# Holding VectorE's side work behind the newest low part of the weights, from the output product to the end of a decoder layer

## The chip, the cores and the metric

The kernel runs on one core of one Trainium2 chip. The metric is the device time of one execution in microseconds (us). Before the change, three runs took 1912.0, 1913.61 and 1914.93 us; the median is 1913.61 us. One further execution was profiled; everything said of single instructions is from it.

## The reference, cut to what matters

One decoder layer on a sequence of 512 rows and 2048 columns, all in float32:

```python
h = rms_norm(x, norm1_g)
proj = h @ w_in                        # 2048 x 6160, feeds two kinds of attention
mix = concatenate([out_a, out_b])      # gated linear attention, dilated attention
x = x + mix @ w_out                    # the output product, 2048 x 2048
h2 = rms_norm(x, norm2_g)
x = x + (silu(h2 @ w_gate) * (h2 @ w_up)) @ w_down    # FFN, hidden size 5632
```

The change touches the last three lines: the output product, the two FFN products (called gate and up below) and the down product.

## The kernel before, in words

**Products in seven.** Two neighbouring 512-column blocks of a weight matrix form a pair, and each pair is computed with seven sub-products in place of eight (Strassen's scheme): PRODUCTS is P1, P5, P6, P3, P7, P2, P4. The activations enter as A11, A12, A21, A22 and as sums S1 to S4 of these; the weights enter as quarters a, b, c, d (512 KB each, loaded into tiles wa, wb, wc, wd). P1, P3 and P2 take one quarter as it is; P5, P6, P7 and P4 need a difference of two quarters, which VectorE makes (`Pair.source`, L298). Each sub-product runs over groups g of 256 rows: four in the output product, in gate and up, and in most of the down product, which is cut into three parts of 4, 4 and 3 groups. There are 2 pairs in the output product, 11 in gate and up, 6 in the down product.

**High and low parts.** TensorE multiplies in a rounded format (fp32r), so each operand is split into a high part (rounded copy) and a low part (the remainder). For weights, ScalarE makes the high part `wh` (L376) and VectorE the low part `wl` = source minus high (L380); both come from a pool with two buffers each (`hpool`). One item of the stream (one sub-product, one group) is twelve matmuls of 512 columns at L405: first eight with `wh`, then four with `wl`. The activations are split the same way into tiles called AA or AS (A11, A12, A22 and S1 to S4; 28 buffers in `apool`): ScalarE writes the high half (L198), VectorE the low half (L199, `Operand.split`).

**The stream.** `stream` walks all items. While it writes down item k it first writes the high part of item k+1, the weight sum of item k+2, the low part of item k+1 (and notes that instruction in `recent["low"]`), then the matmuls of item k; after the eighth matmul it calls `step()`, which releases a share of the background work: splits, sums of activations, loads. `later(n, fn)` puts a closing, a residual addition or a transpose n items further on.

**What sets the order.** Tile's scheduler places the instructions of PE (TensorE), ACT (ScalarE), DVE (VectorE), SP (the DMA queue of the sync engine) by its own estimate of when each can run; each engine then executes its list strictly in that order. `tc.issue_after(ins)` adds one constraint: what is traced inside the block stands behind `ins` on its own engine. The kernel before uses it for the closings of the first pairs of the input product (`behind=True`, L337) and for the sums in `sums_job` (L1464 to L1474).

**Side work on VectorE** from the output product on, beside weight sums and low parts: low halves of splits (L199), sums of activation rows (L223 to L236 in `Operand.build`, L1231 to L1241, L1321 in `kept_job`), closings that add a PSUM accumulator to a saved seed (L339 without and L343 with a row scale), residual additions (`residual`, L1287, L1290, L1293, with the old x loaded into tiles q and k at L1283), the product of silu(gate) and up (L1432), and 32x32-block transposes of the result (L1404). PE also transposes tiles with an identity matrix (L1099) in the output product.

Of the kernel before, what the change touches and what calls it, by code (L numbers as in the profile page):

```python
# [131 lines left out]
def block_kernel(ctx: ExitStack, tc: tile.TileContext, ins, out):  # L132
# [52 lines left out]
    recent = {}  # L185
    done = set()


    class Operand:

# [5 lines left out]
        def split(self, name, g, src):  # L196
            a = apool.tile([P, 2, 2, 256], F32R, name=nm("A" + name), tag="A")
            nc.scalar.copy(a[:, :, 0, :], src)  # L198
            nc.vector.tensor_tensor(  # L199
                a[:, :, 1, :], src, a[:, :, 0, :].bitcast(F32), op=ALU.subtract  # L200
            )
            self.t[name, g] = a

        def half_split(self, which, name, g, src):
# [10 lines left out]
        def build(self, g, r11, r21, r12, r22):  # L215

            get = lambda r: r() if callable(r) else r
            tt = nc.vector.tensor_tensor
            r11 = get(r11)
            self.split("A11", g, r11)  # L220
            yield
            r22 = get(r22)
            self.split("A22", g, r22)  # L223
            yield
            r21 = get(r21)
            tt(r22, r21, r22, op=ALU.add)
            self.split("S1", g, r22)
            yield
            tt(r21, r11, r21, op=ALU.subtract)
            tt(r11, r22, r11, op=ALU.subtract)  # L230
            self.split("S2", g, r11)
            yield
            r12 = get(r12)
            tt(r11, r12, r11, op=ALU.subtract)
            self.split("S4", g, r11)
            yield  # L236
            self.split("S3", g, r21)
            yield
            self.split("A12", g, r12)
            yield  # L240
# [29 lines left out]
    def halves(t):  # L270
        return t.rearrange("p (b a) -> p b a", b=2)
# [1006 lines left out]
    def residual(tiles, acc_, rows, c0, src, late=False):  # L1278

        res, adds = [], []  # L1280
        for m in range(2):
            r = work(("q", "k")[m])
            load(r, src(rows[m], c0))  # L1283
            if late:
                res.append(tiles[m])
                adds.append(
                    lambda m=m, r=r: nc.vector.tensor_tensor(tiles[m], tiles[m], r, op=ALU.add)  # L1287
                )
            elif tiles is None:
                nc.vector.tensor_tensor(halves(r), unfolded(acc_[m]), halves(r), op=ALU.add)  # L1290
                res.append(r)
            else:
                nc.vector.tensor_tensor(tiles[m], tiles[m], r, op=ALU.add)  # L1293
                res.append(tiles[m])
        return res, adds

    kept_n = {}
# [1 line left out]
    def kept_job(op, kept):  # L1299
        tt = nc.vector.tensor_tensor  # L1300
        sums = {
            "S3": ("t1", "t0", "t1", ALU.subtract), "S2": ("t1", "r1", "t1", ALU.subtract),
            "S1": ("t0", "t1", "t0", ALU.add), "S4": ("t1", "r0", "t1", ALU.subtract),
        }
        parts = {"A11": "t0", "S3": "t1", "S1": "t0", "S2": "t1", "A12": "r0", "S4": "t1", "A22": "r1"}
        have = lambda n: (n[0], int(n[1])) in kept
        for word in KEPT.split():
            for one in word.split("+"):
                name, *g = one.split(".")
                split = name in parts and one[0] != "="  # L1310
                name = name.strip("=")
                g = int(g[0])
                needs = [parts[name]] if split else sums[name][:3]
                while not all(have(n) for n in needs):
                    yield
                at = lambda n: kept[n[0], int(n[1])][g - 2]
                if split:
                    op.split(name, g, at(parts[name]))
                else:
                    d, a, b, how = sums[name]  # L1320
                    tt(at(d), at(a), at(b), op=how)  # L1321
            yield

    def final_out(second):
# [51 lines left out]
    opn = Operand(4)  # L1376
    tops = [xn_d[2], xn_d[3], xn_d[6], xn_d[7]]
    bots = [xn_d[0], xn_d[1], xn_d[4], xn_d[5]]
    pair(opm, rows_mix, ocol(0), ocol(512), final_out(0), scripted(step, OUT))
    pair(opm, rows_mix, ocol(1024), ocol(1536), final_out(1), paced([1] * 28))  # L1380


    rows_n = [(512, 0), (768, 256), (1536, 1024), (1792, 1280)]
# [15 lines left out]
    def turned_store(tiles, half, j):  # L1399

        dst = turned_d[j][half].rearrange("q (k i) n -> i (q k) n", i=32)
        for m in range(2):
            d = work(("oT", "PT")[m])
            nc.vector.transpose(d, tiles[m])  # L1404
            for a in range(4):
                store(
                    dst[:, :, m * P + 32 * a : m * P + 32 * a + 32],
# [7 lines left out]
    def final_ffn(j):  # L1415
        ups = {}

        def final(half, which, tiles, acc_):
# [4 lines left out]
            for m in range(2):  # L1423
# [5 lines left out]
                else:  # L1429
                    s = tiles[m]  # L1430
                    nc.scalar.activation(s, s, AF.Silu)
                nc.vector.tensor_tensor(up[m], up[m], s, op=ALU.mult)  # L1432
            def rest():
                if j in turned_d:
                    turned_store(up, half, j)
# [72 lines left out]
    for j in range(11):  # L1508
        pair(
            opn, rows_n, w_gate[:, j], w_up[:, j], final_ffn(j),  # L1510
            paced(paces.get(j, ())), tok_scale, before=lambda j=j: before_ffn(j),
        )


# [45 lines left out]
    for i in range(3):  # L1560
        g0 = 4 * i
        rows_d = [(512 * (g0 + g), 512 * (g0 + g) + 256) for g in range(opd[i].groups)]
        for np_ in range(2):
            lead = np_ == 1 and i < 2
            pair(
                opd[i], rows_d, w_down[:, 2 * np_], w_down[:, 2 * np_ + 1],
                final_down(i, np_), paced(renewal if lead else closing if i < 2 else ()),
                before=(
                    (lambda i=i: background.append(down_jobs(i + 1))) if lead
                    else (lambda: later(6, lambda: background.extend(last_sums))) if (i, np_) == (0, 0) else None  # L1570
# [63 lines left out]
```

## Time and profile before

| | us |
|---|---|
| median of three runs | 1913.61 |
| the profiled execution's own time | 1913.48 |
| its span, first to last instruction | 1911.7 |
| PE busy | 1897.4 |
| DVE busy | 1675.1 |
| ACT busy | 1070.1 |

The output product's first matmul stands at about 545 us, gate and up run from about 702 to 1500 us, the down product from there to 1908 us. In rows of the profile, PE is TensorE's matmuls, PEld its weight loads, DVE VectorE, ACT ScalarE, and SPq the queue that issues DMAs. In a timeline a row has the start, the duration (of the whole row where xcount is over 1), engine, line, operation, tiles and, in brackets, how long the engine was idle before it and what released it. A row of windows has, for each engine, busy time and the number of instructions in brackets. A matmul's start is exact; its end is modelled, and neighbours overlap.

### The profile page before, as it was taken

The numbers are of one execution on the slowest core, as the hardware profiler recorded it, in microseconds if no ns is written. First come the engines' busy times: TensorE is split into PE (matmuls) and PEld (weight loads), VectorE is DVE, ScalarE is ACT, GpSimd is POOL, SyncE is SP. The second block draws the span as 40 slices with busy tenths as digits, with TensorE's granted clock in tenths as the row PEclk, the third lists the DMA queues.
The fourth block names the chain that finished last, engine by engine and source line by source line (L and its number), as shares of the span: only waits on it lengthen the run. The fifth ranks groups of instructions, "written<-read, shape, count | busy, mean of one in ns | idle before, by whom it ended". The sixth has DMA issues, their size and how long they took to land.

```text
span 1911.7 us, 25301 instructions
## 1 busy us (share of the span) xinstructions
PE 1897.4 (99%) x9002; PEld 1644.5 (86%) x9002; DVE 1675.1 (88%) x1956; ACT 1070.1 (56%) x1567; POOL 13.1 (1%) x22
## 2 busy tenths in 40 slices
PE   9999999999999999999999999999999999999999
PEld 7888888888888888888888888888888888888887
DVE  8898797778799999988888888888889989979987
ACT  8654564666776665544544544444546546546543
POOL 0000010000000000000000000000000000000000
PEclk9999999999999999999999999999999999999999
DMA  9637455444536563465465465464466776855761
GB/s 341 209 111 250 147 168 181 144 152 157 188 122 226 162 218 124 124 182 167 136 193 170 121 196 157 129 198 147 141 198 200 213 263 213 278 203 182 237 221 66
DMA packets 246806, 345.73 MB, mean 181 GB/s; under 512 B 107718, under 2 KB 154607, under 8 KB 246680
## 3 DMA queue, kind: packets, MB, share of 16 engines
q1 hardware_dynamic: 246392, 343.99, 55.9%
q8 instruction: 70, 1.15, 0.2%
q14 instruction: 56, 0.46, 0.1%
q10 hardware_dynamic: 288, 0.14, 0.0%
HBM read 286.10 MB, written 60.31 MB: 181 GB/s over the span
## 4 chain that ended last, share of the span: by engine, by line
PE 81%; DVE 7%; DMA 3%; issue 3%; ACT 1%; SPq 0%; DVEq 0%; ACTq 0%
PE acc L405 76%; DVE wl L380 3%; DVE wa L298 1%; PE bank L1003 1%; PE bank L979 1%; DMA q<-y_d 1%; DVE AS L199 1%; PE bank L996 0%; DVE AA L199 0%; DVE seed L1287 0%; DMA wd<-in_w_down 0%; PE bank L1099 0%; PE bank L918 0%; PE bank L901 0%; DMA xn_d<-oT 0%
## 5 line engine op out<-in xcount | busy, mean ns | idle before, releaser
L405 PE MATMUL acc<-wh,AS 128*128 128x512 f32 x3008 | 710.9, 379 | 0.0
L405 PEld LDWEIGHTS acc<-wh,AS 128*128 128x128 f32 x3008 | 568.3, 189 | 81.4 <-ACT wh L376 0.9
L376 ACT CAST wh<-wa 128x1024 fp32r<-128x1024 f32 x376 | 394.4, 1049 | 403.8 <-PE acc L405 367.3
L405 PE MATMUL acc<-wh,AA 128*128 128x512 f32 x2256 | 533.5, 379 | 0.2 <-ACT wh L376 0.2
L380 DVE TENSOR_TENSOR wl<-wa,wh 128x1024 fp32r<-128x1024 f32 x376 | 456.5, 1216 | 57.9 <-ACT wh L376 46.2
L405 PEld LDWEIGHTS acc<-wh,AA 128*128 128x128 f32 x2256 | 426.2, 189 | 61.0 <-ACT wh L376 0.6
L405 PE MATMUL acc<-wl,AS 128*128 128x512 f32 x1504 | 393.7, 384 | 4.3 <-DVE wl L380 4.2
L405 PEld LDWEIGHTS acc<-wl,AS 128*128 128x128 f32 x1504 | 280.8, 189 | 53.0 <-DVE wl L380 12.0
L405 PE MATMUL acc<-wl,AA 128*128 128x512 f32 x1128 | 295.1, 384 | 0.3
L405 PEld LDWEIGHTS acc<-wl,AA 128*128 128x128 f32 x1128 | 211.1, 189 | 34.3 <-DVE wl L380 3.4
L376 ACT CAST wh<-wb 128x1024 fp32r<-128x1024 f32 x94 | 98.6, 1049 | 121.1 <-PE acc L405 118.9
L376 ACT CAST wh<-wc 128x1024 fp32r<-128x1024 f32 x94 | 98.6, 1049 | 119.6 <-PE acc L405 103.9
L376 ACT CAST wh<-wd 128x1024 fp32r<-128x1024 f32 x94 | 98.6, 1049 | 90.4 <-PE acc L405 75.4
L380 DVE TENSOR_TENSOR wl<-wd,wh 128x1024 fp32r<-128x1024 f32 x94 | 114.4, 1219 | 32.1 <-ACT wh L376 28.8
L298 DVE TENSOR_TENSOR wa<-wc,wa 128x1024 f32<-128x1024 f32 x94 | 114.3, 1220 | 30.9 <-DMA wc<-in_w_gate 19.1
L380 DVE TENSOR_TENSOR wl<-wc,wh 128x1024 fp32r<-128x1024 f32 x94 | 114.5, 1219 | 26.7 <-ACT wh L376 26.1
L380 DVE TENSOR_TENSOR wl<-wb,wh 128x1024 fp32r<-128x1024 f32 x94 | 114.3, 1216 | 9.0 <-ACT wh L376 7.3
L298 DVE TENSOR_TENSOR wb<-wd,wb 128x1024 f32<-128x1024 f32 x94 | 114.1, 1216 | 0.4
L298 DVE TENSOR_TENSOR wa<-wb,wa 128x1024 f32<-128x1024 f32 x94 | 113.6, 1211 | 0.8
L298 DVE TENSOR_TENSOR wa<-wd,wa 128x1024 f32<-128x1024 f32 x94 | 112.9, 1215 | 0.1
L343 DVE SCALAR_TENSOR_TENSOR seed<-acc,rs,seed 128x512 f32<-128x512 f32 x96 | 70.3, 745 | 15.8 <-PE acc L405 14.6
L324 ACT ACTIVATE seed<-acc,rs 128x512 f32<-128x512 f32 x96 | 60.8, 682 | 5.1 <-PE acc L405 5.1
(319 smaller groups left out, 1264.5 us busy)
## 6 DMA issues: line engine op xcount, KB each, us to landing
wa<-in_w_gate SPq DMA_DIRECT2D x44, 512.0 KB, 3.3
wb<-in_w_up SPq DMA_DIRECT2D x44, 512.0 KB, 6.0
wd<-in_w_up SPq DMA_DIRECT2D x44, 512.0 KB, 4.3
wc<-in_w_gate SPq DMA_DIRECT2D x44, 512.0 KB, 3.3
wa<-in_w_in SPq DMA_DIRECT2D x24, 512.0 KB, 4.9
wc<-in_w_in SPq DMA_DIRECT2D x24, 512.0 KB, 3.4
wb<-in_w_in SPq DMA_DIRECT2D x24, 512.0 KB, 5.2
wd<-in_w_in SPq DMA_DIRECT2D x24, 512.0 KB, 4.9
```

The costliest lines, as they stand in the source:

```text
L199: nc.vector.tensor_tensor(a[:, :, 1, :], src, a[:, :, 0, :].bitcast(F32), op=ALU.subtract)
L298: nc.vector.tensor_tensor(src, other, src, op=ALU.subtract)
L324: nc.scalar.activation(halves(t), unfolded(src[m]), AF.Copy, scale=self.scale(half, m))
L343: nc.vector.scalar_tensor_tensor(halves(seed[m]), unfolded(src[m]), self.scale(half, m), halves(seed[m]), op0=ALU.mult, op1=ALU.add,)
L376: nc.scalar.copy(high[k], sources[k])
L380: recent["low"] = nc.vector.tensor_tensor(low[k], sources.pop(k), high[k].bitcast(F32), op=ALU.subtract).ins
L405: nc.tensor.matmul(p.dst[prod][m], a[:, jj, hl, m * P : (m + 1) * P], folded(w[i][:, jj, :]), start=fresh and g == 0 and i == 0 and jj == ...
L979: nc.tensor.matmul(lp[:, :n], qh[:, b * P : (b + 1) * P], kh[:, :n], start=True, stop=True)
L1003: nc.tensor.matmul(op, vh[:, k, :], lgs[b][:, k * P : (k + 1) * P], start=(k == 0), stop=(k == b))
```

## The change

A helper `low_first()` opens `tc.issue_after(recent["low"])`: what is traced inside stands on VectorE behind the newest low part of weights traced so far, that is, the one of the next item. It is put around the low halves of all splits, the sums of activation rows in `Operand.build` and `kept_job`, the residual additions, the product with silu and the transposes of the result. All pairs of the output product, of gate and up and of the down product get `behind=True`, which does the same for their closings. No instruction is added or removed; durations and shapes stay.

```diff
+    def low_first():
+
+        return tc.issue_after(recent["low"])
...
         def split(self, name, g, src):
             a = apool.tile([P, 2, 2, 256], F32R, name=nm("A" + name), tag="A")
             nc.scalar.copy(a[:, :, 0, :], src)
-            nc.vector.tensor_tensor(
-                a[:, :, 1, :], src, a[:, :, 0, :].bitcast(F32), op=ALU.subtract
-            )
+            with low_first():
+                nc.vector.tensor_tensor(
+                    a[:, :, 1, :], src, a[:, :, 0, :].bitcast(F32), op=ALU.subtract
+                )
...
-            tt(r22, r21, r22, op=ALU.add)
+            with low_first():
+                tt(r22, r21, r22, op=ALU.add)
...
             if late:
                 res.append(tiles[m])
-                adds.append(
-                    lambda m=m, r=r: nc.vector.tensor_tensor(tiles[m], tiles[m], r, op=ALU.add)
-                )
-            elif tiles is None:
-                nc.vector.tensor_tensor(halves(r), unfolded(acc_[m]), halves(r), op=ALU.add)
-                res.append(r)
+
+                def add(m=m, r=r):
+                    with low_first():
+                        nc.vector.tensor_tensor(tiles[m], tiles[m], r, op=ALU.add)
+
+                adds.append(add)
             else:
-                nc.vector.tensor_tensor(tiles[m], tiles[m], r, op=ALU.add)
-                res.append(tiles[m])
+                with low_first():
+                    if tiles is None:
+                        nc.vector.tensor_tensor(
+                            halves(r), unfolded(acc_[m]), halves(r), op=ALU.add
+                        )
+                    else:
+                        nc.vector.tensor_tensor(tiles[m], tiles[m], r, op=ALU.add)
+                res.append(r if tiles is None else tiles[m])
...
-    pair(opm, rows_mix, ocol(0), ocol(512), final_out(0), scripted(step, OUT))
-    pair(opm, rows_mix, ocol(1024), ocol(1536), final_out(1), paced([1] * 28))
+    pair(opm, rows_mix, ocol(0), ocol(512), final_out(0), scripted(step, OUT), behind=True)
+    pair(opm, rows_mix, ocol(1024), ocol(1536), final_out(1), paced([1] * 28), behind=True)
...
-            nc.vector.transpose(d, tiles[m])
+            with low_first():
+                nc.vector.transpose(d, tiles[m])
...
-                nc.vector.tensor_tensor(up[m], up[m], s, op=ALU.mult)
+                with low_first():
+                    nc.vector.tensor_tensor(up[m], up[m], s, op=ALU.mult)
...
-            paced(paces.get(j, ())), tok_scale, before=lambda j=j: before_ffn(j),
+            paced(paces.get(j, ())), tok_scale, before=lambda j=j: before_ffn(j), behind=True,
...
                 final_down(i, np_), paced(renewal if lead else closing if i < 2 else ()),
+                behind=True,
```

The same wrapping is put around the other sums of `Operand.build` and those of `kept_job`. The scheduler works out all lists anew, so other instructions move too. Three places on VectorE follow (numbers after a tile's name tell its instances apart).

The first place is the first pair of the down product, about 1509 to 1518 us. On VectorE there stood before, from one low part to the third after it:

```order
L380 TENSOR_TENSOR wl_2342_13047<-wa_2336_13021,wh_2340_13043 128x1024
L1404 STREAM_TRANSPOSE oT_2350_13086<-seed_2244_12564 128x512
L298 TENSOR_TENSOR wa_2329_12996<-wb_2353_13104,wa_2329_12996 128x1024
L380 TENSOR_TENSOR wl_2349_13076<-wa_2341_13045,wh_2347_13071 128x1024
L298 TENSOR_TENSOR wa_2336_13021<-wb_2360_13130,wa_2336_13021 128x1024
L298 TENSOR_TENSOR wa_2341_13045<-wb_2364_13151,wa_2341_13045 128x1024
L1404 STREAM_TRANSPOSE PT_2351_13092<-seed_2250_12590 128x512
L380 TENSOR_TENSOR wl_2354_13107<-wa_2322_12961,wh_2352_13102 128x1024
```

And on VectorE between the same low parts now (L388 is the low part, L306 the weight sum, L204 the low half of a split, L1420 the transpose):

```order
L388 TENSOR_TENSOR wl_2342_13047<-wa_2336_13021,wh_2340_13043 128x1024
L204 TENSOR_TENSOR AA12_2344_13059<-T_2326_12985,AA12_2344_13059 128x2x256
L204 TENSOR_TENSOR AA12_2346_13064<-qT_2331_13008,AA12_2346_13064 128x2x256
L388 TENSOR_TENSOR wl_2349_13076<-wa_2341_13045,wh_2347_13071 128x1024
L1420 STREAM_TRANSPOSE oT_2350_13086<-seed_2244_12564 128x512
L306 TENSOR_TENSOR wa_2329_12996<-wb_2353_13104,wa_2329_12996 128x1024
L388 TENSOR_TENSOR wl_2354_13107<-wa_2322_12961,wh_2352_13102 128x1024
```

Two weight sums and a transpose left the stretch ahead of wl_2354, and two splits that stood further ahead came in.

The second place is the last pair, about 1850 to 1859 us, where tiles q and k hold rows loaded by DMA for the residual addition. On VectorE before:

```order
L380 TENSOR_TENSOR wl_2894_15953<-wa_2888_15928,wh_2892_15949 128x1024
L298 TENSOR_TENSOR wa_2888_15928<-wb_2903_16001,wa_2888_15928 128x1024
L1290 TENSOR_TENSOR q_2900_15987<-acc_2821_15543,q_2900_15987 128x512
L380 TENSOR_TENSOR wl_2899_15975<-wa_2893_15951,wh_2897_15971 128x1024
L1290 TENSOR_TENSOR k_2901_15990<-acc_2822_15544,k_2901_15990 128x512
L298 TENSOR_TENSOR wa_2893_15951<-wb_2906_16020,wa_2893_15951 128x1024
L380 TENSOR_TENSOR wl_2904_16004<-wa_2898_15973,wh_2902_15999 128x1024
```

And on VectorE there now (L1297 and L1303 are residual additions):

```order
L388 TENSOR_TENSOR wl_2894_15953<-wa_2888_15928,wh_2892_15949 128x1024
L1297 TENSOR_TENSOR seed_2839_15626<-seed_2839_15626,q_2890_15941 128x512
L306 TENSOR_TENSOR wa_2888_15928<-wb_2903_16001,wa_2888_15928 128x1024
L388 TENSOR_TENSOR wl_2899_15975<-wa_2893_15951,wh_2897_15971 128x1024
L1297 TENSOR_TENSOR seed_2843_15647<-seed_2843_15647,k_2891_15943 128x512
L306 TENSOR_TENSOR wa_2893_15951<-wb_2906_16020,wa_2893_15951 128x1024
L1303 TENSOR_TENSOR q_2900_15987<-acc_2821_15543,q_2900_15987 128x512
L388 TENSOR_TENSOR wl_2904_16004<-wa_2898_15973,wh_2902_15999 128x1024
```

The additions to the seeds now follow two or three low parts later; the loads into q and k can be issued only after these additions have read the tiles, and the addition q_2900 stands directly ahead of wl_2904.

The third place is the third item of the output product, about 549 to 556 us, where the attention's last tiles (cr) are still being finished. On VectorE before:

```order
L380 TENSOR_TENSOR wl_980_5213<-wa_969_5174,wh_978_5209 128x1024
L1136 SCALAR_TENSOR_TENSOR og_962_5141<-acc_759_4177,rs1_102,og_962_5141 128x512
L199 TENSOR_TENSOR AS3_983_5236<-top_963_5144,AS3_983_5236 128x2x256
L298 TENSOR_TENSOR wa_966_5156<-wb_988_5263,wa_966_5156 128x1024
L1147 TENSOR_TENSOR cr_981_5223<-cr_981_5223,og_962_5141 128x512
L1234 TENSOR_TENSOR top_886_4756<-qT_971_5186,top_886_4756 128x512
L298 TENSOR_TENSOR wa_969_5174<-wb_996_5301,wa_969_5174 128x1024
L1147 TENSOR_TENSOR cr_982_5224<-cr_982_5224,og_962_5141 128x512
L380 TENSOR_TENSOR wl_986_5247<-wa_979_5211,wh_984_5243 128x1024
L380 TENSOR_TENSOR wl_989_5266<-wa_985_5245,wh_987_5261 128x1024
```

And on VectorE now, up to the same addition cr_982 (L1155):

```order
L388 TENSOR_TENSOR wl_980_5213<-wa_969_5174,wh_978_5209 128x1024
L1144 SCALAR_TENSOR_TENSOR og_962_5141<-acc_759_4177,rs1_102,og_962_5141 128x512
L204 TENSOR_TENSOR AS3_983_5236<-top_963_5144,AS3_983_5236 128x2x256
L388 TENSOR_TENSOR wl_986_5247<-wa_979_5211,wh_984_5243 128x1024
L1155 TENSOR_TENSOR cr_981_5223<-cr_981_5223,og_962_5141 128x512
L306 TENSOR_TENSOR wa_966_5156<-wb_988_5263,wa_966_5156 128x1024
L388 TENSOR_TENSOR wl_989_5266<-wa_985_5245,wh_987_5261 128x1024
L1155 TENSOR_TENSOR cr_982_5224<-cr_982_5224,og_962_5141 128x512
```

Both low parts now stand ahead of cr_982, which PE's transposes of cr wait for; in PE's list six of these eight transposes stand between two of the four matmuls with wl_986 and the other two.

More of the change, by code (lines that the diff above doesn't have):

```diff
@@ L225, in build @@
             r21 = get(r21)
-            tt(r22, r21, r22, op=ALU.add)
+            with low_first():
+                tt(r22, r21, r22, op=ALU.add)
             self.split("S1", g, r22)
             yield
-            tt(r21, r11, r21, op=ALU.subtract)
-            tt(r11, r22, r11, op=ALU.subtract)
+            with low_first():
+                tt(r21, r11, r21, op=ALU.subtract)
+                tt(r11, r22, r11, op=ALU.subtract)
             self.split("S2", g, r11)
@@ L233, in build @@
             r12 = get(r12)
-            tt(r11, r12, r11, op=ALU.subtract)
+            with low_first():
+                tt(r11, r12, r11, op=ALU.subtract)
             self.split("S4", g, r11)
@@ L1320, in kept_job @@
                     d, a, b, how = sums[name]
-                    tt(at(d), at(a), at(b), op=how)
+                    with low_first():
+                        tt(at(d), at(a), at(b), op=how)
             yield
@@ L1403, in turned_store @@
             d = work(("oT", "PT")[m])
-            nc.vector.transpose(d, tiles[m])
+            with low_first():
+                nc.vector.transpose(d, tiles[m])
             for a in range(4):
@@ L1431, in final @@
                     nc.scalar.activation(s, s, AF.Silu)
-                nc.vector.tensor_tensor(up[m], up[m], s, op=ALU.mult)
+                with low_first():
+                    nc.vector.tensor_tensor(up[m], up[m], s, op=ALU.mult)
             def rest():
```

## The prediction

> **What bounds the kernel now.** I read the page first, then the windows of the stages, the waits, and the timeline where time is lost. TensorE is the bound:
>
> ```profile
> span 1911.7 us, 25301 instructions
> PE 1897.4 (99%) x9002; PEld 1644.5 (86%) x9002; DVE 1675.1 (88%) x1956; ACT 1070.1 (56%) x1567; POOL 13.1 (1%) x22
> ```
>
> PE counts as busy for 99% of the span, so its busy time can't show what is lost. The number of matmuls in a stretch can. These windows count the L405 matmuls alone:
>
> ```profile
> 566.00:667.00 101.00, 97.21 (x441) 82.28 (x441) 1.00 0.56 182
> 895.00:1440.00 545.00, 545.00 (x2526) 477.24 (x2526) 1.00 0.54 163
> 1457.00:1540.00 83.00, 81.18 (x373) 69.75 (x372) 1.00 0.71 222
> 1610.00:1682.00 72.00, 71.68 (x326) 60.40 (x325) 1.00 0.72 242
> 1755.00:1790.00 35.00, 34.92 (x161) 29.70 (x161) 1.00 0.82 276
> 1855.00:1885.00 30.00, 29.77 (x137) 25.25 (x136) 1.00 0.13 42
> ```
>
> In gate and up (895 to 1440) 2526 matmuls take 545 us, 0.2158 us each, and nothing is lost there. At that pitch the 373 matmuls of 1457 to 1540 need 80.5 us of 83: 2.5 lost. In the same way 72 − 326 x 0.2158 = 1.6, 35 − 34.7 = 0.3, and 30 − 29.6 = 0.4. In the output product, 101 − 441 x 0.2158 = 5.8, and from this come PE's 32 transposes:
>
> ```profile
> 566.00:667.00 101.00, 4.15 (x32) 3.74 (x32) 1.00 0.56 182
> 554.45 1.04 PE L1099 MATMUL bank<-mats,cr 128*128 128x128 f32 x8
> 555.31 1.13 PE L405 MATMUL acc<-wl,AA 128*128 128x512 f32 x4
> PEld acc L405 <- DVE wl L380: 4.4, 7, 1.1
> PEld acc L405 <- DVE wl L380: 8.9, 21, 1.4
> ```
>
> By their busy time these cost 4.15 us. By the two timeline rows eight of them put the next matmul off by 0.86 us (554.45 to 555.31), which is 3.5 for the 32; I go by the starts, so 5.8 − 3.5 = 2.3 are lost. The last two rows (waits of 566 to 720 us, and of 1440 to 1905) say to whom: the weight loads of TensorE waited 7 and 21 times for a low part. With one more stall near 718 (below), some 7 to 8 us of 1911.7 are open to this change, under half a per cent. About 0.2% (3.8 us; the three runs lie 2.9 apart) is what a measurement here can tell from no change.
>
> How such a stall arises is seen in VectorE's timeline of the first down pair, and TensorE's beside it:
>
> ```profile
> 1508.54 0.68 DVE L1432 TENSOR_TENSOR seed<-seed,k 128x512 f32<-128x512 f32 x1
> 1509.14 1.22 DVE L380 TENSOR_TENSOR wl<-wa,wh 128x1024 fp32r<-128x1024 f32 x1
> 1510.28 0.70 DVE L1404 STREAM_TRANSPOSE oT<-seed 128x512 f32<-128x512 f32 x1
> 1510.91 1.18 DVE L298 TENSOR_TENSOR wa<-wb,wa 128x1024 f32<-128x1024 f32 x1
> 1512.01 1.21 DVE L380 TENSOR_TENSOR wl<-wa,wh 128x1024 fp32r<-128x1024 f32 x1
> 1513.14 2.35 DVE L298 TENSOR_TENSOR wa<-wb,wa 128x1024 f32<-128x1024 f32 x2
> 1515.41 0.70 DVE L1404 STREAM_TRANSPOSE PT<-seed 128x512 f32<-128x512 f32 x1
> 1516.04 2.31 DVE L380 TENSOR_TENSOR wl<-wa,wh 128x1024 fp32r<-128x1024 f32 x2
> ...
> 1517.27 0.92 PE L405 MATMUL acc<-wl,AS 128*128 128x512 f32 x3 [1.01 <-DVE wl L380]
> ```
>
> VectorE has no gap: back to back an operation on 1024 columns takes 1.13 us (1509.14 to 1510.28), one on 512 takes 0.60 (1508.54 to 1509.14), a transpose 0.63. Two weight sums and a transpose stand ahead of the low part at 1516.04, for which PE is idle 1.01 us. An item of twelve matmuls takes 12 x 0.2158 = 2.59 us; VectorE's share of it, with a weight sum, is 2 x 1.13 = 2.27. The 0.3 left over is too little for any other operation, so splits and additions push the low parts back until an item without a sum comes.
>
> **The change part by part.** No instruction is added; what moves is which of them stands ahead of a low part. In the first place shown of the order, between wl_2342 and wl_2354 there stood a transpose, a sum, a low part, two sums and a transpose: 0.63 + 1.13 + 1.13 + 2.27 + 0.63 = 5.8 us. Now two splits, a low part, a transpose and one sum stand there: 2 x 0.6 + 1.13 + 0.63 + 1.13 = 4.1. That is 1.7 us earlier, more than the 1.01 of idle PE. What left goes behind, to 1540 and later, where nothing is lost. The same holds for the other low parts that PE waits for from 1457 to 1682 and near 1783: less or equal work ahead of each. I take all but 0.2 of the 2.5, about half of what TensorE waited for ScalarE instead (the row below): **−2.3** (bounds −2.5 and −1.0, if the moved work fills the next items). The windows 1610 and 1755: **−1.9**, before what follows.
>
> ```profile
> PEld acc L405 <- ACT wh L376: 0.4, 1, 0.4
> ```
>
> The splits, sums and transposes that now wait have users far off: an A operand is made one pair ahead, dozens of items before its first matmul, so a delay of a few items costs nothing. Closings free PSUM tiles; they move by one item at most of their product's four. FFN: weight sums move ahead of low parts at each pair's start, by 1.13 us; VectorE's idle before low parts covers that:
>
> ```profile
> DVE wl L380 <- ACT wh L376: 62.8, 60, 1.4
> ```
>
> (60 waits from 740 to 1440 us.) Cost nothing; if the cover were gone, up to 1.13 us in each of 11 pairs.
>
> The residual additions are another matter. A load into q or k can be issued only when the addition before it has read the tile, so a held addition delays the next load, on SP's queue, and whatever stands behind it there; and an addition whose rows haven't landed stops VectorE's whole list. The last pair shows it already:
>
> ```profile
> 1849.01 2.40 DVE L380 TENSOR_TENSOR wl<-wa,wh 128x1024 fp32r<-128x1024 f32 x2
> 1849.56 0.40 SPq L1283 DMA_DIRECT2D q<-y_d  x1
> 1850.01 1.32 SPq L1283 DMA_DIRECT2D k<-y_d  x1
> 1851.44 1.22 DVE L298 TENSOR_TENSOR wa<-wb,wa 128x1024 f32<-128x1024 f32 x1
> 1854.12 0.69 DVE L1290 TENSOR_TENSOR q<-acc,q 128x512 f32<-128x512 f32 x1 [1.46 <-DMA q<-y_d]
> 1859.26 1.03 PE L405 MATMUL acc<-wl,AA 128*128 128x512 f32 x4
> q<-y_d SPq DMA_DIRECT2D x15, 256.0 KB, 5.0
> DMA to landing us min/median/max: 2.2/5.0/6.9
> ```
>
> The addition waits 1.46 us for its rows. In the new order (second place) the addition to seed_2839 comes after wl_2894 (the second of the two low parts in the first row, which end at 1851.4), so it ends at 1852.0. SP then issues a store, and the load of q_2900 near 1852.6, not at 1849.56. By the median of 5.0 it lands near 1857.6; q_2900 ends 0.68 later and wl_2904, next in the list, 1.13 after that, at 1859.4. PE needs it at 1859.26. That is 0.2 lost, up to 2.1 with the longest landing of 6.9 and nothing with 2.2; and k_2901 repeats part of it. Against this stand the 0.4 lost there now. I take **0** here (bounds −0.4 and +2.0) and **+0.5** for the same thing at the end of the other tight pair, near 1655 us (bounds 0 and +1.5). Elsewhere the items have room.
>
> The Trainium skill ("DMA: Bandwidth & Descriptors", section on the anatomy of one DMA) prices a DMA on GpSimd's path at 2.0 us plus bytes over 436 GB/s. As an estimate from that page 256 KB would take 2.6 us, half the median of the rows above; by it these two terms would be −0.4 and 0, and the sum 0.9 lower.
>
> **Output product.** VectorE's rows near 630 to 643:
>
> ```profile
> 633.92 0.69 DVE L199 TENSOR_TENSOR AA<-r,AA 128x512 fp32r<-128x512 f32 x1 [1.40 <-ACT AA L198]
> ...
> 642.02 1.22 DVE L380 TENSOR_TENSOR wl<-wa,wh 128x1024 fp32r<-128x1024 f32 x1
> 643.29 0.91 PE L405 MATMUL acc<-wl,AS 128*128 128x512 f32 x3 [0.62 <-DVE wl L380]
> ...
> 718.87 1.13 PE L405 MATMUL acc<-wl,AS 128*128 128x512 f32 x4 [0.75 <-DVE wl L380]
> ```
>
> At 633.92 VectorE idled 1.40 us, because a split stood at the head of its list and its rows had not landed; ten instructions without a gap later PE lacks a low part. The new list puts that split behind the next low part, so the idle time goes, but a weight sum comes in place of the split (1.13 for 0.60: 0.5 more ahead of each low part): 0.9 gained. Of the 0.75 at 718 and the rest of the 2.3 I count 0.4: **−1.3** (bounds −2.3 and 0).
>
> Its start is worse:
>
> ```profile
> 551.48 1.04 ACT L376 CAST wh<-wa 128x1024 fp32r<-128x1024 f32 x1
> 553.45 0.68 DVE L1147 TENSOR_TENSOR cr<-cr,og 128x512 f32<-128x512 f32 x1
> ```
>
> Today cr_982 (553.45) is ready when PE comes to its eight transposes at 554.45 (the row near the top). In the third place of the order wl_986 and wl_989, 2 x 1.13, stand ahead of it; a sum (1.13) and a sum of rows (0.6) leave, so it comes some 0.5 us later by work, and wl_986 must wait for a cast that ends at 552.5, where another 0.5 to 1.5 goes. PE would wait up to 1.5 us. I take **+0.9** (bounds −0.5 and +2.0; it lies nearer to the cast's row, which is fixed by when TensorE frees the buffer).
>
> **The sum** against the profiled execution: −2.3 − 1.9 + 0.5 + 0 − 1.3 + 0.9 = −4.1, so 1913.48 − 4.1 = 1909.4 us. The median of the runs is 0.13 above the profiled time, which I leave out. The end of the kernel does not move: the last closings stand ahead of PE's last matmuls before and after.
>
> **The rivals.**
>
> *The stall moves (no change).* Where VectorE has no gap, putting work behind one low part puts it ahead of the next; only idle time that goes or weight sums that move out of the stretch are a real gain. For it: from 636 to 643 VectorE is full before and after. Against it: after 1540 and 1682 there is room. Then −1.2 at 1457, −0.8 at 1610 and 1755, 0 in the output product but the +0.9: −1.1, 1912.4 us. Chance 0.27.
>
> *Late residual rows (slower).* The additions held behind low parts make five pairs of the down product wait at their last product:
>
> ```profile
> L1290 DVE TENSOR_TENSOR q<-acc,q x5: 678/683/691, 1580.3 to 1854.1; 128x512 f32<-128x512 f32 x5
> ```
>
> At 2.1 us each (landing after 6.9) five pairs cost 10.5; with the −2.3, −1.9 and −0.4 gained elsewhere that is +5.9, 1919.4 us. It decides from 1.7 us per pair on. Against it: only one pair in five waited for such rows before (1.46). Chance 0.09.
>
> *Rows land early (faster).* All landings near the minimum of 2.2 us: −2.3 − 1.9 − 0.4 − 1.3 + 0.9 = −5.0, 1908.5 us. This is what the page's rule would give. Against it: the median of 5.0. Chance 0.12.
>
> *All waits go (faster).* The start costs nothing either, and the output product gains its full 2.3 and the 0.75 at 718: −2.5 − 1.9 − 0.4 − 3.1 = −7.9, 1905.6 us. Chance 0.08.
>
> **How the numbers follow.** My forecast, 1909.4, has 0.44; its own bounds straddle 1909.8, the 0.2% line, and I count 0.32 of it as faster and 0.12 as no change. Faster: 0.32 + 0.12 + 0.08 = 0.52. Within 0.2%: 0.12 + 0.27 = 0.39. Slower: 0.09. The range reaches down to the case in which all waits go, 1905.6, and up past the moved stall (1912.4) by the upper bound of the start (2.0 − 0.9 = 1.1) and 0.5 of the last pair's 2.0: 1914.0; it leaves out most of the slower case.
>
> **What would show it.** Right: the count of L405 matmuls in the stretch of the first down pair at the pitch of 0.2158, and few waits of PEld for wl after 1440; the gap at 1517 gone. The start: PE waiting for the cr addition between 553 and 557. The last pair: VectorE's wait for q rows longer than 1.46. Wrong: PEld's waits for wl unchanged in sum but at other items, or waits for DMA rows in several down pairs.

## The result, and the profile after

The changed kernel is slower. Its median over six runs is 1927.41 us (1924.94 to 1930.93), that of the kernel before, run beside it, 1912.8 us, 14.6 us less. The ratio, formed from the means, is 1.0074 with a 95% interval of 1.006 to 1.0089. The forecast was 1909.4, with a range that ended at 1914.0. The profiled execution took 1926.13 us.

The page of the changed kernel, first the span, then each engine's busy time with its instructions:

```profile
span 1924.3 us, 25274 instructions
PE 1902.8 (99%) x9002; PEld 1642.9 (85%) x9002; DVE 1676.0 (87%) x1956; ACT 1069.2 (56%) x1567; POOL 13.3 (1%) x22
```

The work is the same (DVE 1676.0 us against 1675.1); the span has 12.6 us more. The windows of the matmuls (now L413), over about the same stretches as those shown of before:

```profile
566.20:668.40 102.20, 97.93 (x441) 82.28 (x441) 1.00 0.55 179
895.55:1441.55 546.00, 546.00 (x2530) 477.15 (x2529) 1.00 0.55 163
1457.70:1544.20 86.50, 83.42 (x381) 70.81 (x379) 1.00 0.70 213
1618.40:1690.00 71.60, 71.33 (x323) 60.63 (x324) 1.00 0.72 249
1765.10:1801.00 35.90, 34.84 (x159) 29.79 (x160) 1.00 0.86 283
```

At 0.2158 us a matmul the output product lost 102.2 − 95.2 = 7.0, less 3.5 for the transposes, that is 3.5 us (2.3 before). Gate and up still lost nothing. The first down pair lost 86.5 − 82.2 = 4.3 (2.5 before), the other two windows 1.9 and 1.6 (1.6 and 0.3). From 1440 us on the weight loads waited:

```profile
PEld acc L413 <- DVE wl L388: 16.9, 26, 1.8
PEld acc L413 <- ACT wh L384: 4.6, 6, 1.4
```

Waits for low parts, which the change was to shorten, went from 8.9 to 16.9 us, and waits for ScalarE's casts from 0.4 to 4.6.

A second reading needs no windows: the start of the same matmul (the k-th at that line) in both traces, and how far the two drift apart. It gives for each stretch what the profiled execution lost (+) or gained (−) against the profiled execution of before, in us:

| kernel | 93–707 | 707–1449 | 1449–1586 | 1586–1907 |
|---|---|---|---|---|
| changed | +1.6 | +0.4 | +3.3 | +7.8 |
| splits not held | +0.3 | +0.4 | 0.0 | +4.9 |
| residual additions not held | +0.2 | +0.6 | +4.3 | +7.0 |
| neither held | −0.1 | +0.3 | +0.7 | +0.2 |
| only splits held | +0.7 | −0.6 | +6.7 | +3.2 |
| changed, operand's rows loaded once | +2.6 | +0.3 | −0.9 | +7.8 |
| changed, residual rows loaded once | +5.6 | +0.3 | +3.0 | +1.8 |
| changed, both kinds of rows loaded once | +0.7 | +0.3 | −1.0 | −0.9 |
| before, both kinds of rows loaded once | −1.5 | −0.7 | −1.7 | −0.9 |
| nothing of the down product held | +1.0 | +0.5 | −1.0 | +0.7 |
| only the last pair of gate and up | −1.7 | −0.2 | −0.7 | 0.0 |

(Times of before; the kernels below the first row are those of the experiments.) Of the 13 us, 11 are lost in the down product. The first column is the least sure: "before, both kinds of rows loaded once" and the last row have the order of before on TensorE, VectorE and ScalarE up to 1440 us, and still they show −1.5 and −1.7 there. So the profiled execution of before seems to have been some 1.6 us late in that stretch itself, and the column shows the cost of the change there too small by about as much.

Nor does one execution always stand for its kernel. The profiled one of "splits not held" took 1918.65 us against a median of 1922.45, that of "residual additions not held" 1926.64 against 1920.28, that of "residual rows loaded once" 1924.49 against 1919.25. The table says where time is lost; the medians say how much.

**What happened there.** One place in the first down pair, in the changed kernel: ScalarE, VectorE, the DMA queue and TensorE, in order of time.

```profile
1473.03 0.61 ACT L202 CAST AS<-qT 128x512 fp32r<-128x512 f32 x1
1483.84 0.68 DVE L204 TENSOR_TENSOR AS<-qT,AS 128x512 fp32r<-128x512 f32 x1
1484.10 1.06 ACT L384 CAST wh<-wc 128x1024 fp32r<-128x1024 f32 x1 [1.54 <-DMA wa<-in_w_down]
1484.55 0.33 SPq L1208 DMA_DIRECT2D qT<-S_d  x1
1488.98 0.62 ACT L202 CAST AS<-qT 128x512 fp32r<-128x512 f32 x1 [3.81 <-DMA qT<-S_d]
...
1490.21 1.04 ACT L384 CAST wh<-wc 128x1024 fp32r<-128x1024 f32 x1
1491.30 1.99 PE L413 MATMUL acc<-wh,AA 128*128 128x512 f32 x8 [1.02 <-ACT wh L384]
```

and the same load in the kernel before:

```profile
1473.96 0.68 DVE L199 TENSOR_TENSOR AS<-qT,AS 128x512 fp32r<-128x512 f32 x1
1474.67 0.32 SPq L1200 DMA_DIRECT2D qT<-S_d  x1
1480.81 0.61 ACT L198 CAST AS<-qT 128x512 fp32r<-128x512 f32 x1
```

The low half of a split is the last reader of its staging tile (here qT). In both kernels the next load into the tile is issued 0.03 us after the low half ends: 1474.64 and 1474.67, 1484.52 and 1484.55. The held low half ran 10 us after its high half (1473.64 to 1483.84); the load has landed by 1488.98. ScalarE takes its list in order, so it stood still for 3.81 us ahead of the high half, and the cast of weights behind it (after one more split's, not shown) came 1 us too late for TensorE. From 1440 us on ScalarE waited for rows 21 times, 33.3 us in all (four of its ten groups are shown); in the kernel before it was 4 times and 6.6 us (all three groups):

```profile
ACT AA L202 <- DMA T<-turned_d: 5.0, 2, 3.3
ACT AS L202 <- DMA kT<-S_d: 4.7, 5, 2.3
ACT AS L202 <- DMA qT<-S_d: 4.4, 2, 3.8
...
ACT AA L202 <- DMA oT<-turned_d: 1.6, 1, 1.6
```

```profile
ACT AS L198 <- DMA T<-S_d: 2.6, 1, 2.6
ACT AS L198 <- DMA kT<-S_d: 2.1, 2, 1.1
ACT AA L198 <- DMA kT<-turned_d: 1.9, 1, 1.9
```

The residual additions did the same on VectorE itself: their loads came later, and VectorE stood still for the rows. Near 1590 us, changed kernel:

```profile
1583.83 0.66 SPq L1291 DMA_DIRECT2D q<-x_d  x1
1590.17 0.69 DVE L1303 TENSOR_TENSOR q<-acc,q 128x512 f32<-128x512 f32 x1 [2.73 <-DMA q<-x_d]
...
1592.51 1.21 DVE L388 TENSOR_TENSOR wl<-wa,wh 128x1024 fp32r<-128x1024 f32 x1
1593.78 1.13 PE L413 MATMUL acc<-wl,AA 128*128 128x512 f32 x4 [1.42 <-DVE wl L388]
```

and before:

```profile
1571.69 0.44 SPq L1283 DMA_DIRECT2D q<-x_d  x1
1580.26 0.68 DVE L1290 TENSOR_TENSOR q<-acc,q 128x512 f32<-128x512 f32 x1
```

The load was issued 8.6 us ahead of its addition before, 6.3 after, and VectorE's whole list, low part included, stopped 2.73 us for it.

### The profile page after: what moved, and what is told of

Its sections match the earlier page's. It is cut to its first block, busy times and chain, and to the rows that moved or that the text cites. A ratio compares the mean times of both kernels' runs of the same rounds, so it can differ in the third digit from the quotient of the medians.

```text
span 1924.3 us, 25274 instructions
## 1 busy us (share of the span) xinstructions
PE 1902.8 (99%) x9002; PEld 1642.9 (85%) x9002; DVE 1676.0 (87%) x1956; ACT 1069.2 (56%) x1567; POOL 13.3 (1%) x22
## 4 chain that ended last, share of the span: by engine, by line
PE 72%; DVE 12%; DMA 5%; issue 4%; ACT 1%; SPq 0%; DVEq 0%; ACTq 0%
PE acc L413 67%; DVE wl L388 5%; DVE wa L306 3%; DVE AS L204 1%; PE bank L1011 1%; DMA wc<-in_w_down 1%; PE bank L987 1%; DVE AA L204 1%; DVE wb L306 1%; DMA q<-x_d 1%; PE bank L1004 0%; DMA mix_d<-r 0%; DMA kT<-S_d 0%; DMA top<-mix_d 0%; ACT wh L384 0%
## 5 line engine op out<-in xcount | busy, mean ns | idle before, releaser
L413 PE MATMUL acc<-wh,AS 128*128 128x512 f32 x3008 | 711.3, 379 | 1.6 <-ACT wh L384 1.5
L413 PEld LDWEIGHTS acc<-wh,AS 128*128 128x128 f32 x3008 | 568.0, 189 | 84.3 <-ACT wh L384 3.6
L413 PE MATMUL acc<-wh,AA 128*128 128x512 f32 x2256 | 533.5, 379 | 1.3 <-ACT wh L384 1.3
L388 DVE TENSOR_TENSOR wl<-wa,wh 128x1024 fp32r<-128x1024 f32 x376 | 455.6, 1216 | 84.1 <-ACT wh L384 69.2
L413 PEld LDWEIGHTS acc<-wh,AA 128*128 128x128 f32 x2256 | 426.1, 189 | 62.8 <-ACT wh L384 2.5
L413 PE MATMUL acc<-wl,AS 128*128 128x512 f32 x1504 | 395.4, 385 | 7.0 <-DVE wl L388 6.6
L413 PEld LDWEIGHTS acc<-wl,AS 128*128 128x128 f32 x1504 | 279.1, 189 | 61.9 <-DVE wl L388 21.9
L413 PE MATMUL acc<-wl,AA 128*128 128x512 f32 x1128 | 294.8, 383 | 2.2 <-DVE wl L388 2.0
L413 PEld LDWEIGHTS acc<-wl,AA 128*128 128x128 f32 x1128 | 211.6, 189 | 34.7 <-DVE wl L388 3.8
L388 DVE TENSOR_TENSOR wl<-wc,wh 128x1024 fp32r<-128x1024 f32 x94 | 114.6, 1220 | 34.5 <-ACT wh L384 33.8
L306 DVE TENSOR_TENSOR wa<-wc,wa 128x1024 f32<-128x1024 f32 x94 | 114.2, 1220 | 32.0 <-DMA wc<-in_w_gate 20.5
L388 DVE TENSOR_TENSOR wl<-wd,wh 128x1024 fp32r<-128x1024 f32 x94 | 114.3, 1219 | 25.6 <-ACT wh L384 22.4
L388 DVE TENSOR_TENSOR wl<-wb,wh 128x1024 fp32r<-128x1024 f32 x94 | 114.3, 1217 | 10.3 <-ACT wh L384 9.6
L306 DVE TENSOR_TENSOR wa<-wb,wa 128x1024 f32<-128x1024 f32 x94 | 113.9, 1214 | 0.6
L306 DVE TENSOR_TENSOR wb<-wd,wb 128x1024 f32<-128x1024 f32 x94 | 113.9, 1217 | 0.4
L306 DVE TENSOR_TENSOR wa<-wd,wa 128x1024 f32<-128x1024 f32 x94 | 113.0, 1215 | 0.1
```

Of the source, the lines that this page charges most:

```text
L306: nc.vector.tensor_tensor(src, other, src, op=ALU.subtract)
L388: recent["low"] = nc.vector.tensor_tensor(low[k], sources.pop(k), high[k].bitcast(F32), op=ALU.subtract).ins
L413: nc.tensor.matmul(p.dst[prod][m], a[:, jj, hl, m * P : (m + 1) * P], folded(w[i][:, jj, :]), start=fresh and g == 0 and i == 0 and jj == ...
```

## The experiments

They ran in four groups, each beside the kernel before, which had medians of 1911.31, 1911.42, 1911.97 and 1912.85 us there. Theory L is the reading above; its parts are called S (splits) and R (residual additions) in the first group. Theory M is the rival of the prediction ("the stall moves"), taken further: that the order on VectorE itself sets the loss. Where an expectation speaks of 14 us of waits for residual rows, the sums of the groups are 11.0 in the changed kernel, and 10.9 for both kinds of rows in the one before.

**Splits not held.**

```diff
-            with low_first():
+            if True:
                 nc.vector.tensor_tensor(
                     a[:, :, 1, :], src, a[:, :, 0, :].bitcast(F32), op=ALU.subtract
                 )
```

> The changed kernel, but the low halves of splits are not held any more; all else of the change stays. The changed kernel took 1927.41 us, the one before 1912.8. Theory S (split rows come late): a held low half frees its staging tile (T, qT, kT, oT, PT, v) later, the next rows of the down product's operand are loaded later, ScalarE stops in its list for them, and the cast of weights behind it comes late. Then this kernel gains most: no wait of TensorE for casts from 1460 to 1500, and the splits no longer stand in pairs: about 1918 us (1916 to 1921). Theory R (residual rows come late): the held residual additions cost most; then this kernel stays near 1925 (1923 to 1928). Theory M (the stall only moves): any one part undone gives back its share, here a third to a half: 1921 to 1923.

1922.45 us, ratio 1.0056 (1.0043 to 1.0069). ScalarE's waits for rows of the operand fell from 33.3 to 4.9 us, and the stretch 1449 to 1586 lost nothing. But most of the time stayed: 4.9 us after 1586. S alone is too little, and the median lies where theory M had it (1921 to 1923).

**Residual additions not held.**

```diff
-                    with low_first():
+                    if True:
                         nc.vector.tensor_tensor(tiles[m], tiles[m], r, op=ALU.add)
...
-                with low_first():
+                if True:
                     if tiles is None:
```

> The changed kernel, but the residual additions are not held; all else stays. Theory R: VectorE no longer stops for rows of q and k (waits of 2.73, 3.1 and 1.96 us in the changed kernel), so the losses near 1592 (2.0 us) and 1816 to 1828 (1.9 us) go, and loads queued behind them come earlier: 1920 (1917 to 1923). Theory S: it stays at 1924 to 1928, and the waits of TensorE for casts at 1467 to 1500 (2.7 us in the changed kernel) stand unchanged. Theory M: 1922 to 1926, with the lost time at other items.

1920.28 us, ratio 1.0044 (1.0031 to 1.0058). VectorE's waits for residual rows fell from 11 us to 3.5; ScalarE's for rows stayed at 29. The median is the one that theory R gave, but 9.0 us of the loss stayed: R alone is too little as well.

**Neither held** (both edits).

> The changed kernel with neither splits nor residual additions held; sums of rows, closings, the product with silu and the transposes stay held. Theories S and R together: both costs gone, 1911 to 1914, as before or a little faster. If S and R each hold only a part and the closings or sums cost too (theory C: closings held behind low parts free PSUM and seeds later): 1917 to 1922.

1913.27 us, ratio 1.0011 (1.0003 to 1.002). Here closings, sums, silu products and transposes are still held, and the loss is nearly gone: S and R together, as expected. The 2.0 us that remain are clear of the noise.

**Only splits held** (the kernel before, with one edit).

```diff
+            with low_first():
                 nc.vector.tensor_tensor(
                     a[:, :, 1, :], src, a[:, :, 0, :].bitcast(F32), op=ALU.subtract
                 )
```

> The kernel before with only the low halves of splits held. Theory S: nearly the whole loss comes back, 1920 to 1925 us, with the waits of ScalarE for rows (3.81 us near 1489 in the changed kernel) and those of TensorE for casts behind them. Theory R: 1911 to 1915. Theory M: 1913 to 1917, with waits for low parts that sum to those of before (14.1 us from 540 us on).

1923.03 us, ratio 1.006 (1.0047 to 1.0072). So the change without its splits (11.1), without its residual additions (9.0) and the splits alone (11.7) cost 9 to 12 us each, the whole 14.6: the parts don't add up. That a pair which is late for one reason loses little by the other would explain it, but no run shows it. The number is the one that theory S gave, and it lies outside that of theory M.

**Rows loaded once.** The next four test the path through the loads, by leaving loads out (so they compute with old rows); first the rows of the down product's operand (the arguments that pass `once` down are left out here, in the next cut too):

```diff
-            t = work(tags[count[0] % len(tags)], (P, 2, 256))
+            tag = tags[count[0] % len(tags)]
             count[0] += 1
-            load(t, src[half])
-            return t
+            if once is None or tag not in once:
+                t = work(tag, (P, 2, 256))
+                load(t, src[half])
+                if once is not None:
+                    once[tag] = t
+                return t
+            return once[tag]
```

> The changed kernel, but the rows of the down product's operand are loaded into each staging tile (T, qT, kT, v, oT, PT) only the first time; later splits read the same rows again. It leaves these loads out (nearly all of the 256 KB loads from S_d, turned_d and the like after 1450 us), with the splits held as in the changed kernel. Theory L (a held low half costs because the next load waits for it): ScalarE's waits for rows (33 us in the changed kernel from 1440 us on, 5 us with splits not held) are gone, TensorE waits for casts under 2 us, and the time is that of the kernel with splits not held, 1922.5 (1918 to 1924), since the residual rows still come late. Theory M (the order on VectorE itself costs): no change, 1925 to 1929, with low parts waited for as before.

1922.63 us, ratio 1.0048 (1.0035 to 1.0062). No wait of ScalarE for rows was left, none of TensorE for casts, and the time is that of "splits not held". The order on VectorE was still the held one (18 of its 1956 instructions stand elsewhere), so it is the load that made the split dear.

Then the residual rows:

```diff
-            r = work(("q", "k")[m])
-            load(r, src(rows[m], c0))
+            r = once.get(m) if once is not None else None
+            if r is None:
+                r = work(("q", "k")[m])
+                load(r, src(rows[m], c0))
+                if once is not None:
+                    once[m] = r
```

> The changed kernel, but the residual rows of the down product are loaded into q and k only the first time (the other loads are left out), with the additions held. Theory L: VectorE never waits for rows of q and k (14 us in the changed kernel from 1440 us on), the losses at 1592 and 1816 to 1828 go, and the time is that of the kernel with residual additions not held, 1920.3 (1917 to 1922). Theory M: 1925 to 1929.

1919.25 us, ratio 1.0044 (1.0031 to 1.0057): again the same as not holding the additions, 1920.28. Place by place it agrees. By the starts (times of before) the changed kernel lost 2.0 us from 1586 to 1600, 1.2 from 1700 to 1755 and 2.1 from 1800 to 1830; without held additions, and with their rows loaded once, these three places lost nothing. The first down pair, 1449 to 1539, goes by the splits: +1.5 in the changed kernel, −1.0 without held splits, −2.1 with the operand's rows loaded once, but +3.0 and +1.7 in the two kernels where the residual rows alone were spared.

Then both, in the changed kernel and in the one before:

> The changed kernel with both kinds of rows loaded only the first time (both loads left out). Theory L: nothing is left of the loss of 14.6 us; only the order on VectorE differs from the next kernel, and the 2 to 4 us forecast for the better order come out: 1906 to 1911, and 1 to 4 us faster than the next kernel. Theory M: still 8 to 14 us slower than the next kernel.

> The kernel before with both kinds of rows loaded only the first time (the same loads left out). It is the measure for the last one. Its waits for rows were few (14 us, of which little reached TensorE), so both theories expect 1908 to 1912 us, 0 to 3 us faster than the kernel before.

1913.4 us, ratio 1.0012 (1.0003 to 1.0021), and 1908.95 us, ratio 0.9987 (0.9979 to 0.9996). So of the 14.6 us about 10 come through the two kinds of loads. But 4.45 us remain between these two kernels, where theory L expected a gain of 1 to 4; that part of it fell. Their waits for low parts from 1440 us on, changed kernel first, are alike:

```profile
PEld acc L413 <- DVE wl L388: 6.3, 14, 0.9
```

```profile
PEld acc L405 <- DVE wl L380: 6.2, 18, 0.9
```

With no late rows the new order on VectorE is worth nothing in the down product. By the starts, 3.1 of the 3.8 us between the two traces lie ahead of 1449 us. Leaving loads out also takes traffic away (315.6 MB are moved in place of 345.7), and the kernel before gained 2.5 us with it; the next two runs keep every load.

**How far the hold reaches.** `low_first(n)` takes the low part n items older than the newest, for splits and residual additions alone.

```diff
-    def low_first():
+    lows = []
+
+    def low_first(back=0):
...
-        return tc.issue_after(recent["low"])
+        return tc.issue_after(lows[max(0, len(lows) - 1 - back)])
```

> The changed kernel, but the low halves of splits and the residual additions stand behind the low part three items (7.8 us) older than the newest; all else stays. In the trace a held low half ran 6.2 us (first down pair), 12.6 us and 9.9 us (later pairs) after its high half, in the kernel before 2.6, 4.5 and 3.7. Theory L (the staging tile and q, k come free late, the next rows land late): three items back most of the extra lag is gone, and with it most of the loss: 1912 to 1917 us, ScalarE's waits for rows from 1440 us on under 15 us (33 in the changed kernel). Theory M (any constraint of this kind disturbs the order): 1920 to 1927.

> The same, one item (2.6 us) older. Theory L: the loss lies between the changed kernel and the last one: 1918 to 1924 us, ScalarE's waits for rows 15 to 30 us. Theory M: as the changed kernel, 1925 to 1929.

Three back: 1919.8 us, ratio 1.0039 (1.0027 to 1.0052), ScalarE's waits for rows 8.7 us. In the down product it lost 2.3 us, not 11, as theory L had it; but in its profiled execution 3.8 were lost ahead of 707 us, where VectorE waited 2.8 for a residual row of the output product, and the median missed the expected range. One back: 1927.83 us, ratio 1.0084 (1.007 to 1.0097), no better than the newest. ScalarE's waits for rows fell to 21 us, as theory L had it, but VectorE's for residual rows stayed (11.6 against 11.0), TensorE's for low parts rose from 16.9 to 20.8, and the down product lost 13.6 us in place of 11. Here theory M's number came true; whether its reason did, no run shows.

**Nothing of the down product held** (so too at its residual additions, and no `behind=True` there).

```diff
-    opd = [Operand(4), Operand(4), Operand(3)]
+    opd = [Operand(4, False), Operand(4, False), Operand(3, False)]
```

> The changed kernel with nothing held that belongs to the down product (the splits of its operand, its residual additions, its closings); the output product and gate and up stay as changed. It asks where the 4.5 us come from that remained with both loads left out. Theory P (the output product and gate and up got slower by themselves, about 2.1 and 0.6 us by the starts of the matmuls): 1913 to 1916 us. Theory Q (all the loss is in the down product): 1910 to 1912 us.

1914.61 us, ratio 1.0014 (1.0005 to 1.0023): 2.6 us are lost outside the down product (theory P). In its first down pair it gained 1.2 us by the starts (1449 to 1539). The waits there, 1445 to 1545 us:

```profile
PEld acc L414 <- DVE wl L389: 1.0, 3, 0.4
PEld acc L414 <- ACT wh L385: 1.4, 2, 1.0
```

```profile
PEld acc L405 <- DVE wl L380: 3.2, 4, 1.4
PEld acc L405 <- ACT wh L376: 0.4, 1, 0.4
```

The second two rows are the kernel before's: the waits for low parts fell by 2.2, those for casts rose by 1.0. The idle 1.01 us ahead of 1517.27 is gone, and the wait at 1458 too.

**Only the last pair of gate and up** (closings, silu products, transposes), with all else as before.

```diff
+                with low_first() if j == 10 else ExitStack():
                     nc.vector.tensor_tensor(up[m], up[m], s, op=ALU.mult)
```

> The kernel before with only three things of the change, and those only in the last pair of gate and up (1440 to 1530 us): its closings, its products with silu and its transposes are held; no split, no residual addition, no sum, nothing in the output product. The trace of the kernel with nothing of the down product held had 1.0 us of waits for low parts there in place of 3.2. If that gain belongs to these instructions alone: 1.0 to 1.5 us faster than the kernel before by the starts of the matmuls, 1909.5 to 1911.5 in the median, at the edge of what can be told apart. If the stall only moves: 1911 to 1913.

1911.28 us, ratio 0.9991 (0.9982 to 1.0). By the starts it gained 0.7 us in that pair; the stall at 1458 (1.07 us by the starts) stayed, that at 1517 went. It is the best version found that keeps every load, and not clearly better than the kernel before; 1911.28 lies in both expected ranges and decides nothing between them.

## Why the prediction was wrong, step by step

- **What bounds the kernel** was right: TensorE, with 7 to 8 us open. Nothing could be gained beyond that; much could be lost, and the range did not say so.
- **"A delay of a few items costs nothing"** for splits is the step that failed. I followed the split's result, whose user is far off, and not its input. The rows were in the trace of before: qT's load 0.03 us behind its split, then 6 us to the cast. The held split delayed that load, the load stopped ScalarE, and the cast behind it came late. The term was put at nothing; without held splits or without their loads some 5 us of the loss go (1927.41 to 1922.45 and 1922.63).
- **"A few items"** was wrong too. From the end of a high half to the start of its low half 2.6 us went by in the first down pair before and 6.2 after (means of 19 splits each), and in 1590 to 1690 4.5 and 12.6 (24 and 26). With the hold three items (7.8 us) older it was 8.3 there. The scheduler had run the low halves ahead of where the code traces them; the hold pins them there, while the high halves and loads stay early.
- **The late residual rows** were named as a rival, at 2.1 us a pair and with a chance of 0.09. The mechanism was right, and the price nearly so: 2.0, 1.2 and 2.1 us at the ends of three pairs (after VectorE's waits of 2.73, 1.33 and 1.96 us), though not in all five; undone, 7 us come back in the medians. The forecast did count that the load behind a held addition is issued later, but only in the last pair (0) and near 1655 (+0.5), and of the others it said "Elsewhere the items have room". That is the second step that failed: the two places counted lost nothing (−0.6 and −0.4), the three others did.
- **First down pair, −2.3.** Measured +1.5 up to 1539 us: −1.1 up to 1460, +2.9 from there to 1500, −0.3 after it. Both stalls that were to go went, those at 1458 and at 1517. The counted 1.7 us of work less was real: from the start of wl_2342 to that of wl_2354 it is 6.9 us before and 5.2 after. But the sums and the transpose that moved stood ahead of the next low part, and there, at 1523.02, TensorE waited 0.68 us; and the casts made late by the splits cost the 2.9, of which 0.2 is left with the operand's rows loaded once. With both loads out of the way the pair came to −2.1, only 0.5 better than its counterpart (−1.7). From 1539 to 1586, where nothing was to be lost, 1.7 went (1.1 with both loads out). The windows 1610 and 1755, −1.9 together, lost 0.7 and 1.1.
- **Last pair, 0:** −0.6. The number was near, but the sign named for it did not come: VectorE waited 0.68 us for q's rows there, not longer than 1.46.
- **Start of the output product, +0.9.** Right, by the wait that was named. TensorE waited for the cr addition, 0.81 us by the starts (0.80 in "nothing of the down product held", which has this order too):

```profile
554.96 0.87 PE L1107 MATMUL bank<-mats,cr 128*128 128x128 f32 x6 [0.64 <-DVE cr L1155]
...
636.36 1.99 PE L413 MATMUL acc<-wh,AS 128*128 128x512 f32 x8 [0.58 <-ACT wh L384]
```

  Against the profiled execution of before it hardly shows (+0.3 from 543 to 566 us), because that one lost 2.05 us there, 1.65 ahead of the seed's transposes and 0.40 for a cast; four other traces with its order on TensorE (splits not held, neither held, before with both rows loaded once, only the last pair) lost 0.9 to 1.4 at these transposes and nothing for a cast. Against those four the changed kernel's start costs 0.9 to 1.5 us.
- **Output product, −1.3.** Measured +1.1 from 566 to 718 us, and more against the two traces of unchanged order, which lie at −1.0 and −1.4. The idle 1.40 ahead of the split went, and a new one came: the held residual addition stopped VectorE for 2.26 us, and at 636.36 (above) a cast was late.

```profile
628.39 0.69 DVE L1303 TENSOR_TENSOR q<-acc,q 128x512 f32<-128x512 f32 x1 [2.26 <-DMA q<-in_x]
```

  This wait alone does not explain the 2.6 us outside the down product: with neither splits nor residual additions held VectorE waited for no such row, and the stretch still came out at +0.7; with splits held and residual additions not, it came out at −0.8. Which of the held instructions cost time there was not tested apart, and stays open.
- **"Rows land early"**, the rival with a chance of 0.12, did not come. The residual rows, on which it rests, took 5.8 us (q from x_d) and 6.2 (q from y_d) in the median from issue to landing between 1440 and 1800 us. By the price of a DMA on GpSimd's path in the Trainium skill ("DMA: Bandwidth & Descriptors", section on the anatomy of one DMA) the prediction's estimate for 256 KB was 2.6 us. Only the quickest loads here agree with it, such as qT's from S_d with a median of 2.6; the late one of these shown above took 4.4 (1484.55 to 1488.98).

## What to carry to other kernels

Before an operation is moved later, ask for each tile that it reads who is waiting to write it: a load issued 0.03 us behind the operation's end is the sign that a delay of the operation delays the load by as much. Then look at which in-order list takes the landed rows, and what stands behind them there. And a constraint that is written relative to where code is traced can reach much further than one item, if the scheduler had hoisted that code.

## What the runs showed of the hardware

A long wait of TensorE can cost nearly twice its length. The kernel with the operand's rows loaded once, near 1592 us:

```profile
1587.95 1.89 PE L413 MATMUL acc<-wh,AA 128*128 128x512 f32 x8
1591.99 2.07 PE L413 MATMUL acc<-wl,AA 128*128 128x512 f32 x4 [2.15 <-DVE wl L388]
1593.85 2.64 PE L413 MATMUL acc<-wh,AS 128*128 128x512 f32 x8
1596.33 1.03 PE L413 MATMUL acc<-wl,AS 128*128 128x512 f32 x4
```

After 2.15 us of waiting, the next twelve matmuls took 4.34 us (1591.99 to 1596.33) in place of 2.59: 1.75 us more. Those in the middle stood 0.426 us apart, half the pace, and the granted clock from 1592 to 1596 was 0.58. The windows of the kernel with only splits held, after waits of 0.48 and 1.76 us within 3 us, show the granted clock beside it (third column from the right):

```profile
1536.00:1540.00 4.00, 1.83 (x8) 0.95 (x6) 4.00 (x4) 1.02 (x2) 0.00 (x0) 0.97 0.43 131
1540.00:1541.00 1.00, 0.93 (x2) 0.84 (x3) 0.95 (x2) 0.97 (x2) 0.00 (x0) 0.50 0.00 0
```

The profile of the residual rows loaded once had it after 1.67 us for a seed at 546; a wait of 1.42 us (1593.78 in the changed kernel) did not bring it on, nor did one of 1.59 (638.19 in the kernel held three items back), so these runs give no length from which it sets in. The Trainium skill ("TensorE: Matmul & The Clock Gate", Part 1) tells of this half rate after an idle window of about 3.4 us. Here shorter waits were enough; in the first row above TensorE was busy for 1.83 of 4 us. The slowest run of the changed kernel, 1930.93 us, had a mean granted clock of 0.998, the other five 1.0. So a single profiled time is a poor measure of a kernel with long waits.
